# First FFN block of a two-layer transformer kernel: the last six blocks of inner units by quarter products, with the layer norms in the order of the finished tiles

## The chip, the cores and the metric

The kernel runs on one core of one Trainium2 chip, as one launch. The metric is device time in microseconds (us) of that launch; smaller is better. Time before: 1941.02 us, the median of 3 runs (1931.21 to 1941.77).

## What is computed

Two networks follow each other on a sequence of 512 tokens of width 1024. The first has two layers of sliding-window attention, retention and gated linear attention. The second has two layers, each a mixer and a gated FFN with a short convolution, and each followed by a layer norm over the sum with the residual. The change is in the first FFN of the second network, and what comes after it is the odd mixer.

```
def conv_ffn(x, w_up, conv_w, conv_b, w_down):       # D_FF = 2816 = 22 blocks of 128
    a, g = jnp.split(x @ w_up, 2, axis=-1)
    g = conv(g, conv_w) + conv_b                      # depthwise, 3 taps, causal
    return (jax.nn.gelu(g) * a) @ w_down

for l in range(2):
    y = even_mixer(x, ...) if l % 2 == 0 else odd_mixer(x, ...)
    x = layer_norm(alpha * x + y, ln_g[l, 0], ln_b[l, 0])
    y = conv_ffn(x, ffn_w_up[l], ...)
    x = layer_norm(alpha * x + y, ln_g[l, 1], ln_b[l, 1])
```

All matmuls of this part are float32 products made of float32r pieces: an operand is split into a rounded high part and the rest (`hi`, `lo`), and one product costs three matmuls (hi·hi, hi·lo, lo·hi).

## The kernel before

**Tiling.** Tokens stand in four tiles of 128 (t = 0 to 3). The residual sum `z[t]` is 128x1024 and is updated in two column halves n = 0, 1 of 512. `hT` holds the transposed, split input of a stage (8 blocks of 128 features). The 22 blocks of inner units go in three parts of 8, 8 and 6 (`for part, (nch, quart) in enumerate(...)`, line 1481). For each part, the "up" products of at most four blocks at a time are made (the loop `for q0 in range(0, nch, 4)`; 24 matmuls of 128x512 for the g half of each block and 24 for the a half, by `fsteps`, lines 1060 to 1062), then evacuated by `ev_g` (lines 1575 to 1579) and `ev_a` (line 1582), and then the "down" product of the part is added into `z`.

**Two forms of the down product.** With `quart` set (parts 0 and 1) `quarters` (lines 1496 to 1502) builds from each pair of blocks four combined operands, and `down_quart` (from line 1505) forms the product of a pair of blocks, two halves of tokens and two halves of columns as 7 products instead of 8 (a Winograd form of the 2x2 block scheme). Its weights come as three buffers `bq` per pair (x, y, s). A buffer is loaded by SP (line 1517), split into a `w` tile by ACT and DVE (lines 243 and 244, called from `operand`), and then, where `then` is given, the next combination is made in place by a DMA that adds to it, issued on POOL's queue (line 1525). Buffer y goes through four contents in that way, x through three, s holds one. Products run in the order 0, 1, 4, 2, 5, 6, 3 (lines 1547 to 1549); `take` (line 1537) adds a finished one to `z`. Products 0, 5, 6 and 3 share two PSUM banks (`X`), so that some of them hold sums that are taken several times.

Without `quart` (part 2, six blocks) ACT and DVE only split the activations (lines 1588 and 1589), twelve weight tiles are loaded (`load_w`, lines 226 and 227), and `down_part` makes 6 x 3 matmuls for each of four tiles and two halves: 144 matmuls (`dsteps`, lines 231 to 233), each tile's sum taken by line 1621.

**The end of the block.** `ln_stats` (line 1142) reads each half of a finished tile, and `ln_apply` combines the statistics (line 1146), has POOL raise the variance to the power -1/2 (`rpow`, lines 281 and 282), and writes the normed tile by two DVE instructions per half (lines 1151 and 1152). Then `finish` puts off two transposes (`to_T`, line 274, with its split into `hT` by lines 243 and 244) and stores the tile. `start_odd` loads the first weights of the odd mixer (8 tiles of 128x312, three DMA pieces each) and gives a function `Vd(t)` with 24 matmuls of 128x312 for tile t. Before the change the work stands in this order: half n = 0 of tiles 3, 2, 1, 0; half n = 1 of tiles 3, 2, 1, each with its layer norm; Vd(3); half n = 1 of tile 0; Vd(2), Vd(1), Vd(0).

**What sets the order.** Each engine runs its instructions in the order of its own queue and waits for semaphores. The order within a queue is set when the program is built, by a scheduler that moves instructions of the source text past each other. Weight tiles `w` rotate through nine slots (`wslots`: six, and three more inside the FFN, `more_w`), the four `raw` buffers and the eight `bq` buffers are rings of their own. A split of a weight waits until the matmuls that used its slot are done.

## Time and profile before

| | |
|---|---|
| three timed runs | 1931.21, 1941.02, 1941.77 us (median 1941.02) |
| the profiled execution, its own time | 1936.26 us |
| span of the profile | 1934.5 us |
| TensorE (PE) busy | 1874.2 us, 97% |
| VectorE (DVE) busy | 1251.6 us, 65% |
| ScalarE (ACT) busy | 828.1 us, 43% |
| GpSimd (POOL) busy | 260.1 us, 13% |
| the chain that ended last, PE's share | 65% |

The profile is one execution. Its rows have a start in us from the span's start, a length, the engine, the source line and what was written from what. A bracket at the end of a row is the idle time of the engine just before it, and who ended it. In tables by stretch, "x" is the count of instructions, "PEclk" the granted share of TensorE's full clock of 2.4 GHz. A matmul's length overlaps with the next one's, so its price is the distance from start to start.

### The profile page before, as it was taken

The page shows a single profiled execution, that of the slowest core. Times are in us where ns is not written, and L with a number is a line of the kernel's source. Part 1 is how long each engine was busy: PE and PEld are TensorE (multiplying, and loading weights), DVE is VectorE, ACT ScalarE, POOL GpSimd, SP SyncE. Part 2 cuts the span into 40 slices and gives each one's busy share as a digit, 9 for nine tenths or more (in the row PEclk, how much of TensorE's full clock was granted, in tenths as well). Part 3 has the DMA queues.
Part 4 walks back from the last instruction along what each step waited for, and adds up shares of the span by engine and source line. Part 5 has one row for each costly group of instructions (what it writes and reads, how often), then busy time and mean ns, then how long its engine had stood idle before and what let it go on. Part 6 is the DMA issues. An engine that isn't in the chain of part 4 may idle for free.

```text
span 1934.5 us, 29305 instructions
## 1 busy us (share of the span) xinstructions
PE 1874.2 (97%) x10144; PEld 1518.6 (79%) x10144; DVE 1251.6 (65%) x3060; ACT 828.1 (43%) x1840; POOL 260.1 (13%) x380
## 2 busy tenths in 40 slices
PE   7899899999999999999999999999999999999997
PEld 4777687877888888868888888788778888888886
DVE  5697886485775244686675674755776776756646
ACT  2432354433463344453443443244665544434341
POOL 3011101012101000101020020101441200200101
PEclk9999999999999999999999999999999999999999
DMA  8535524226124233403373362363114033733632
GB/s 278 173 89 165 150 86 137 86 84 183 44 94 157 73 106 121 153 12 116 117 155 99 91 149 72 117 188 91 42 29 148 24 133 112 154 97 96 134 88 82
DMA packets 139784, 218.76 MB, mean 113 GB/s; under 512 B 21633, under 2 KB 53747, under 8 KB 139636
## 3 DMA queue, kind: packets, MB, share of 16 engines
q1 hardware_dynamic: 130420, 200.11, 33.6%
q0 software_dynamic: 9216, 16.78, 5.2%
q8 instruction: 80, 1.31, 0.3%
q14 instruction: 68, 0.56, 0.1%
HBM read 207.20 MB, written 14.09 MB: 114 GB/s over the span
## 4 chain that ended last, share of the span: by engine, by line
PE 65%; DVE 7%; issue 6%; POOL 3%; DMA 2%; ACT 1%; POOLq 0%; DVEq 0%; SPq 0%; ACTq 0%
PE mm L1060 10%; PE mm L1062 10%; PE mm L1061 9%; PE mm L231 6%; PE mm L233 6%; PE mm L232 6%; PE t L1095 1%; PE o L1547 1%; PE o L1549 1%; PE o L1548 1%; DMA bq<-in_ffn_w_down_dram 1%; PE mm L1547 1%; PE mm L1549 1%; PE mm L1548 1%; PE t L274 1%
## 5 line engine op out<-in xcount | busy, mean ns | idle before, releaser
L227 DVE TENSOR_TENSOR w<-raw,w 128x512 fp32r<-128x512 f32 (+4 forms) x496 | 307.5, 638 | 140.1 <-ACT w L226 138.4
L226 ACT CAST w<-raw 128x512 fp32r<-128x512 f32 (+4 forms) x504 | 284.5, 575 | 239.8 <-PE mm L233 55.9
L1060 PE MATMUL mm<-hT,w 128*128 128x512 f32 x920 | 366.6, 399 | 0.2
L1062 PE MATMUL mm<-hT,w 128*128 128x512 f32 x920 | 361.6, 394 | 0.1
L1061 PE MATMUL mm<-hT,w 128*128 128x512 f32 x920 | 360.7, 392 | 0.0
L231 PE MATMUL mm<-w,hT 128*128 128x512 f32 (+3 forms) x704 | 278.3, 396 | 1.4 <-ACT hT L243 1.3
L233 PE MATMUL mm<-w,hT 128*128 128x512 f32 (+3 forms) x704 | 262.5, 373 | 0.4 <-DVE hT L244 0.4
L232 PE MATMUL mm<-w,hT 128*128 128x512 f32 (+3 forms) x704 | 261.0, 371 | 0.1
L1060 PEld LDWEIGHTS mm<-hT,w 128*128 128x128 f32 x920 | 172.9, 188 | 39.7 <-ACT w L226 1.8
L1062 PEld LDWEIGHTS mm<-hT,w 128*128 128x128 f32 x920 | 172.7, 188 | 39.4 <-DVE w L227 1.3
L1061 PEld LDWEIGHTS mm<-hT,w 128*128 128x128 f32 x920 | 172.9, 188 | 35.2
L231 PEld LDWEIGHTS mm<-w,hT 128*128 128x128 f32 x704 | 138.9, 198 | 31.0 <-issue 6.5
L233 PEld LDWEIGHTS mm<-w,hT 128*128 128x128 f32 x704 | 138.8, 197 | 21.9 <-DVE hT L244 1.3
L232 PEld LDWEIGHTS mm<-w,hT 128*128 128x128 f32 x704 | 139.4, 198 | 16.8 <-issue 2.0
L1525 POOL DMA_DIRECT2D bq<-in_ffn_w_down_dram x64 | 56.6, 1280 | 413.0 <-DVE w L244 401.7
L1576 DVE SCALAR_TENSOR_TENSOR g<-mm,cw,g 128x511 f32<-128x511 f32 x44 | 33.0, 749 | 108.5 <-ACT g L1575 108.4
L243 ACT CAST w<-bq 128x512 fp32r<-128x512 f32 x112 | 69.0, 621 | 65.1 <-DMA bq<-in_ffn_w_down_dram 20.2
L1090 ACT ACTIVATE E<-E,nm 128x128 f32<-128x128 f32 (+3 forms) x128 | 71.6, 560 | 45.0 <-DVE nm L1089 42.3
L244 DVE TENSOR_TENSOR w<-bq,w 128x512 fp32r<-128x512 f32 x112 | 75.5, 689 | 15.4 <-ACT w L243 14.8
L1582 DVE TENSOR_TENSOR ge<-ge,mm 128x512 f32<-128x512 f32 x44 | 30.1, 685 | 67.6 <-PE mm L1062 67.5
L1575 ACT ACTIVATE g<-mm,cw 128x512 f32<-128x512 f32 x44 | 34.2, 777 | 79.6 <-PE mm L1062 63.1
L1085 DVE COPY pT<-t 128x512 f32<-128x512 f32 (+3 forms) x84 | 43.0, 512 | 37.8 <-PE t L1280 23.3
(472 smaller groups left out, 3458.3 us busy)
## 6 DMA issues: line engine op xcount, KB each, us to landing
raw<-in_ffn_w_up_dram SPq DMA_DIRECT2D x160, 256.0 KB
rawm<-in_w_mod_dram SPq DMA_DIRECT2D x96, 256.0 KB
raw<-in_w_in_dram SPq DMA_DIRECT2D x80, 256.0 KB
bq<-in_ffn_w_down_dram POOLq DMA_DIRECT2D x64, 256.0 KB, 7.7
raw<-in_ev_w_in_dram SPq DMA_DIRECT2D x48, 256.0 KB
bq<-in_ffn_w_down_dram SPq DMA_DIRECT2D x48, 256.0 KB
raw<-in_w_out_dram SPq DMA_DIRECT2D x32, 256.0 KB
raw<-in_ffn_w_down_dram SPq DMA_DIRECT2D x24, 256.0 KB
```

The lines of the kernel that those rows point to most:

```text
L226: SC.copy(hi, r)
L227: (eng or V).tensor_tensor(lo, r, hi.bitcast(F32), op=OP.subtract)
L231: PE.matmul(ps, hi, w[:, 0, w0:w0 + n], start=first, stop=False)
L232: PE.matmul(ps, hi, w[:, 1, w0:w0 + n], start=False, stop=False)
L233: PE.matmul(ps, lo, w[:, 0, w0:w0 + n], start=False, stop=last)
L243: SC.copy(hi, ps)
L244: V.tensor_tensor(lo, ps, hi.bitcast(F32), op=OP.subtract)
L1060: PE.matmul(ps, wh, hi, start=k == ks[0], stop=False)
L1061: PE.matmul(ps, wh, lo, start=False, stop=False)
L1062: PE.matmul(ps, wl, hi, start=False, stop=k == ks[-1])
L1090: SC.activation(E, E, AF.Exp, scale=scale, bias=nm, accum_out=den)
L1525: GP.dma_start(bufs[name, p], src[then](p), accum_op=OP.add)
```

## The change

For the first FFN only (`l == 0`), part 2 goes by quarters as well, as three pairs of blocks. `down_quart` takes a function `done(t, n)` that it calls after the last take of a half tile, and the layer norm of a tile follows when both its halves are done: tiles 0 and 1 after product 5, tiles 2 and 3 after product 3. `start_odd` and the four `Vd(t)` come after all of it, in the order 0, 1, 2, 3.

```diff
-        for part, (nch, quart) in enumerate(((8, True), (8, True), (6, False))):
+        for part, (nch, quart) in enumerate(((8, True), (8, True), (6, l == 0))):
...
-            def down_quart():
+            def down_quart(done=lambda t, n: None):
...
-                product(1, o2, W, True, True, False, lambda r, ps: take(0, r, False, ps))
+                product(1, o2, W, True, True, False, lambda r, ps: (take(0, r, False, ps), done(r, 0)))
...
-                product(5, o6, X, False, False, True, lambda r, ps: take(1, r, True, ps))
+                product(5, o6, X, False, False, True, lambda r, ps: (take(1, r, True, ps), done(r, 1)))
                 o4 = operand("y")
-                product(6, o7, X, False, False, True, lambda r, ps: take(1, 2 + r, True, ps))
-                product(3, o4, X, False, True, True, lambda r, ps: take(0, 2 + r, False, ps, first))
+                product(6, o7, X, False, False, True, lambda r, ps: (take(1, 2 + r, True, ps), done(2 + r, 1)))
+                product(3, o4, X, False, True, True, lambda r, ps: (take(0, 2 + r, False, ps, first), done(2 + r, 0)))
...
-            if quart:
+            if quart and part < 2:
                 down_quart()
                 c0 += nch
                 continue
             lg = rows(1)
+            if quart:
+                def done(t, n):
+                    if t not in st6:
+                        st6[t] = sm.tile([128, 2, 6], F32, name="st6")
+                        ln_stats(st6[t], z[t], n)
+                        return
+                    ln_stats(st6[t], z[t], n)
+                    ln_apply(st6[t], z[t], lg[0], lg[1], lambda m: finish(t, m))
+                down_quart(done)
+                Vd = start_odd()
+                for t in range(4):
+                    flush(("h", t))
+                    drain(Vd(t))
+                flush()
+                c0 += nch
+                continue
```

How the rows move. The first place is DVE's queue at the start of the last part's down product in the changed kernel. Tiles `w` are weight operands, `ge` the activations of the last pair of blocks, `act_11198` the operand that the first product needs of that pair, `bq_11747` to `bq_11751` the three y buffers and `bq_11838` the first x buffer; "waits DMASW" is a wait for an adding DMA of POOL's queue, and each of these splits follows a cast of the same buffer on ACT's queue, which stands in the same order.

```order
L244 TENSOR_TENSOR w_11800<-bq_11747,w_11800 128x512 [waits DMASW0_49,Activation_49]
L244 TENSOR_TENSOR w_11804<-bq_11749,w_11804 128x512 [waits DMASW1_49,Activation_49]
L1582 TENSOR_TENSOR ge_11634<-ge_11634,mm_11702 128x512 [waits PE_49]
L244 TENSOR_TENSOR w_11808<-bq_11751,w_11808 128x512 [waits DMASW2_49,Activation_49]
L1497 TENSOR_TENSOR ge_11603<-ge_11634,ge_11603 128x256 [waits DVE_49]
L244 TENSOR_TENSOR w_11844<-bq_11838,w_11844 128x512 [waits Activation_49]
L1500 SCALAR_TENSOR_TENSOR g0_11728<-ge_11603 128x256 [waits DVE_49]
L244 TENSOR_TENSOR act_11198<-ge_11603,act_11198 128x512 [waits Activation_49]
```

In part two of the program before, the same place has only the first two of four such splits behind the evacuation of line 1582 and none of them ahead of it; in the changed kernel all three y splits for product 4 stand ahead of the first product's last operand.

The second place is DVE's queue where the layer norms meet the first weights of the odd mixer (`w<-raw 128x312`, line 227). Before, around the norms of tiles 3 and 2 (`z_8189`, `z_8188`):

```order
L227 TENSOR_TENSOR w<-raw,w 128x312 [waits DMAHW1_49,DMAHW7_49,DMAHW0_49,Activation_49]
L227 TENSOR_TENSOR w<-raw,w 128x312 [waits DMAHW3_49,DMAHW4_49,DMAHW2_49,Activation_49]
L1621 SCALAR_TENSOR_TENSOR z_8189<-z_8189,mm 128x512 [waits PE_49]
L1142 BN_STATS st_11797<-z_8189 128x6 [waits DVE_49]
L1146 BN_AGGR mv<-st_11797 128x2 [waits DVE_49]
L1151 SCALAR_TENSOR_TENSOR z_8189<-z_8189,mv,lng 128x512 [waits DVE_49]
```

In the changed kernel, at the end of the norm of tile 2 and through that of tile 3:

```order
L1152 SCALAR_TENSOR_TENSOR z_8188<-z_8188,rstd,lnb 128x512 [waits DVE_49]
L1142 BN_STATS st_11996<-z_8189 128x6
L227 TENSOR_TENSOR w<-raw,w 128x312 [waits DMAHW5_49,DMAHW3_49]
L1146 BN_AGGR mv<-st_11996 128x2 [waits DVE_49]
L227 TENSOR_TENSOR w<-raw,w 128x312 [waits DMAHW7_49,DMAHW6_49,DMAHW0_49]
L1151 SCALAR_TENSOR_TENSOR z_8189<-z_8189,mv,lng 128x512 [waits DVE_49]
L1151 SCALAR_TENSOR_TENSOR z_8189<-z_8189,mv,lng 128x512
L1152 SCALAR_TENSOR_TENSOR z_8189<-z_8189,rstd,lnb 128x512 [waits DVE_49,Pool_49]
L1152 SCALAR_TENSOR_TENSOR z_8189<-z_8189,rstd,lnb 128x512 [waits DVE_49]
L227 TENSOR_TENSOR w<-raw,w 128x312 [waits DMAHW3_49,DMAHW2_49,DMAHW1_49]
L227 TENSOR_TENSOR w<-raw,w 128x312 [waits DMAHW7_49,DMAHW6_49,DMAHW5_49]
```

Before, three of the eight splits stand ahead of the first norm and the other five are spread between the norms. Now one stands ahead of the norms (in tile 0's), the second and third come in tile 3's norm, the fourth and fifth behind it, and the last three come between the splits of `hT` that follow.

The third place is PE's queue after the last product, where Vd(0) begins (`mm_12118` is Vd(0), `mm_12161` Vd(1), `w_12066` and `w_12073` the first two of the eight weight tiles):

```order
L231 MATMUL mm_12118<-w_12066,hT_82 128x312 [waits Activation_49]
L232 MATMUL mm_12118<-w_12066,hT_82 128x312
L274 MATMUL t_12119<-con_72,z1_8187 128x128 [waits DVE_49,PE_49]
L274 MATMUL t_12119<-con_72,z1_8187 128x128 x3
L233 MATMUL mm_12118<-w_12066,hT_82 128x312
L231 MATMUL mm_12118<-w_12073,hT_82 128x312
L231 MATMUL mm_12161<-w_12066,hT_82 128x312 [waits Activation_49]
L274 MATMUL t_12126<-con_72,z1_8187 128x128 [waits DVE_49]
L274 MATMUL t_12126<-con_72,z1_8187 128x128 x3
L232 MATMUL mm_12161<-w_12066,hT_82 128x312
L232 MATMUL mm_12118<-w_12073,hT_82 128x312 [waits DVE_49]
```

Here PE's queue, which held 18 matmuls of a down product between two tiles' Vd before, holds only transposes and Vd matmuls, and the second weight's low part (the last row) stands ahead of 89 of the 96 Vd matmuls. The queue of PE has 7736 rows for 7755 before.

## Rows read from the trace of the kernel before

**Rows 1.** The page's head: span, busy time, share and instructions of PE and DVE.
```profile
span 1934.5 us, 29305 instructions
PE 1874.2 (97%) x10144; PEld 1518.6 (79%) x10144; DVE 1251.6 (65%) x3060; ACT 828.1 (43%) x1840; POOL 260.1 (13%) x380
```

**Rows 2.** Busy time by stretch: down product of part two, up of part three, its down, Vd.
```profile
core 0: us, PE busy (x) PEld busy (x) DVE busy (x) ACT busy (x) POOL busy (x), PEclk, DMA share, GB/s
1112.60:1151.00 38.40, 38.40 (x167) 31.16 (x167) 29.91 (x49) 18.68 (x33) 10.57 (x12) 1.00 0.77 159
1151.00:1217.38 66.38, 66.38 (x291) 54.23 (x290) 31.07 (x55) 25.86 (x48) 0.00 (x0) 1.00 0.29 87
1217.38:1246.61 29.23, 29.23 (x127) 23.61 (x126) 19.81 (x32) 5.42 (x10) 3.14 (x4) 1.00 0.36 103
1246.61:1270.20 23.59, 22.80 (x147) 20.34 (x146) 19.58 (x39) 10.10 (x23) 3.78 (x7) 1.00 0.38 123
```

**Rows 3.** PE's waits from 1100 to 1300 us: total, times, longest.
```profile
PE mm L233 <- DVE hT L244: 0.4, 1, 0.4
PE mm L231 <- ACT hT L243: 0.2, 1, 0.2
```

**Rows 4.** PE in time: first matmuls of both down products, ends of both, last Vd.
```profile
1112.42 0.40 PE L1547 MATMUL o<-w,act 128*128 128x512 f32 x1
...
1151.28 0.39 PE L1060 MATMUL mm<-hT,w 128*128 128x512 f32 x1
...
1217.38 0.39 PE L231 MATMUL mm<-w,act 128*128 128x512 f32 x1
...
1266.78 0.30 PE L231 MATMUL mm<-w,hT 128*128 128x312 f32 x1
...
1270.20 0.39 PE L1060 MATMUL mm<-hT,w 128*128 128x512 f32 x1
```

**Rows 5.** DVE groups from 1217.38 to 1270.2 us: count, busy us, mean ns, idle before.
```profile
L1151 DVE SCALAR_TENSOR_TENSOR z<-z,mv,lng 128x512 f32<-128x512 f32 x8 | 5.7, 748 | 0.1
L1152 DVE SCALAR_TENSOR_TENSOR z<-z,rstd,lnb 128x512 f32<-128x512 f32 x8 | 5.7, 747 | 1.8 <-POOL rstd L282 1.8
L1142 DVE BATCH_NORM_STATS2 st<-z 128x6 f32<-128x512 f32 x8 | 5.5, 692 | 0.2
L1621 DVE SCALAR_TENSOR_TENSOR z<-z,mm 128x512 f32<-128x512 f32 x8 | 5.5, 682 | 5.9 <-PE mm L233 5.9
L244 DVE TENSOR_TENSOR hT<-t,hT 128x512 fp32r<-128x512 f32 x8 | 5.4, 683 | 1.5 <-ACT hT L243 1.5
L1146 DVE BATCH_NORM_AGGREGATE mv<-st 128x2 f32<-128x12 f32 x4 | 0.8, 207 | 0.1
```

**Rows 6.** DVE in time: splits of weights, and the last evacuation of part two.
```profile
1108.45 4.88 DVE L244 TENSOR_TENSOR w<-bq,w 128x512 fp32r<-128x512 f32 x7 [0.19 <-ACT w L243]
1113.24 0.68 DVE L1582 TENSOR_TENSOR ge<-ge,mm 128x512 f32<-128x512 f32 x1
...
1254.42 0.87 DVE L227 TENSOR_TENSOR w<-raw,w 128x312 fp32r<-128x312 f32 x2
```

**Rows 7.** PE transposes from 1217.38 to 1270.2 us: the group's busy time.
```profile
L274 PE MATMUL t<-con,z 128*128 128x128 f32 x32 | 4.8, 273 | 0.0
```

**Rows 8.** POOL's adding DMAs: issues in time, then all 64, issue to landing.
```profile
1109.44 2.64 POOL L1525 DMA_DIRECT2D bq<-in_ffn_w_down_dram  x3 [12.96 <-DVE w L244]
...
DMA to landing us min/median/max: 3.9/7.7/10.8
```

**Rows 9.** ACT in time, part two: the two casts that an adding DMA held up.
```profile
1117.13 0.62 ACT L243 CAST w<-bq 128x512 fp32r<-128x512 f32 x1 [0.57 <-DMA bq<-in_ffn_w_down_dram]
1119.37 0.62 ACT L243 CAST w<-bq 128x512 fp32r<-128x512 f32 x1 [1.61 <-DMA bq<-in_ffn_w_down_dram]
```

**Rows 10.** Stretches around two pauses of PE in the first network.
```profile
160.50:164.00 3.50, 1.50 (x9) 1.34 (x10) 2.09 (x7) 0.47 (x1) 1.20 (x2) 0.88 0.02 8
164.00:167.50 3.50, 3.50 (x7) 2.10 (x8) 2.26 (x10) 0.00 (x0) 0.00 (x0) 0.50 0.22 75
167.50:171.00 3.50, 3.50 (x16) 2.89 (x14) 1.77 (x4) 0.38 (x1) 0.84 (x2) 0.65 0.47 116
...
181.50:185.00 3.50, 1.90 (x13) 1.40 (x11) 3.13 (x10) 0.37 (x1) 0.00 (x0) 1.00 0.48 150
185.00:188.50 3.50, 3.31 (x17) 2.17 (x18) 3.50 (x8) 0.62 (x1) 0.00 (x0) 1.00 0.55 128
```

## The prediction

> **What bounds the kernel now.** I read the page's head first: TensorE (PE) is busy for 97% of the span and DVE for 65% [rows 1]. Then the busy times of the stretches around the change: in the last part's up product, its down product and Vd, PE leaves 0.8 us of 119 us free, and the table of PE's waits has 0.6 us in 200 us [rows 2, 3]. So in this place the kernel is bound by PE's work, and every matmul taken away is worth its distance from start to start, as long as no wait opens. Next to that the reader should see how far DVE is loaded: 31.07 us of 66.38 in the up stretch, but 19.58 of 23.59 in the stretch with the layer norms and Vd [rows 2]. There DVE has little left, and whatever moves onto it there, or is squeezed into a shorter stretch, can become the bound. Last I read the adding DMAs, since the changed part waits for twelve of them, which the trace shows in parts one and two alone [rows 8, 9].
>
> **The work of PE.** The down product of part two is 168 matmuls from 1112.42 to 1151.28 [rows 4], 0.231 us each. The last part had 144 such matmuls and gets 7 x 3 x 2 x 3 = 126: 18 fewer, **-4.2 us**. The transposes (32, 4.8 us [rows 7]) and the 96 matmuls of Vd stay. Vd's price is 24 matmuls from 1266.78 to 1270.20 [rows 4], 0.1425 us each.
>
> **Edits that I cost at nothing.** `quarters` gives DVE and ACT more to do for three pairs of blocks in the up stretch, where DVE is free for 35 of 66 us [rows 2]; were that cover gone, the operands of the first product would come later, which is the next step. Eight `bq` loads now stand in SP's queue ahead of most of the last part's up weights. In part two the loads stand like that already, and PE had no idle time in its 38.40 us [rows 2]. The twelve weight loads of before become nine loads and twelve adding DMAs of the same size, in stretches with a DMA share of 0.29 to 0.36 [rows 2]. POOL has to issue twelve more DMAs, and the four norms' two POOL steps stand behind them, but the last issue is due two products earlier than the first norm.
>
> **A wait at the first product.** The first product needs the high part of operand m of the last pair after 14 matmuls, 3.2 us. On ACT and DVE the splits for product 4 stand ahead of it, the third of them behind the landing of the third adding DMA (the first place of the order). In part two the corresponding issues begin at 1109.44 and the third of a run of them about 0.7 us after the second [rows 8]; the second stands for the third here, as one of the three is made early in both. That is 2.3 us before the product's start at 1112.42 [rows 4]. The shortest landing is 3.9 us [rows 8], and the casts held up at 1117.13 and 1119.37 [rows 9] show 7 us and more after issue, when four x loads ran beside them; here one does. So the data is there 1.6 to 4.7 us after the product's start. A cast, a split, the evaluation of line 1497 and the cast of m follow, 2.2 us with the lengths of [rows 6, 9]. m is ready at 3.8 to 6.9 us where 3.2 was wanted: a wait of 0.6 to 3.7 us, and nothing if the DMA lands earlier than any did. I take **+2.0 us**, the middle. The Trainium skill, "DMA: Bandwidth & Descriptors", section "Anatomy of one DMA — SWDGE (gpsimd) path", gives a DMA of this path about 2.0 us and its bytes at 436 GB/s, an estimate of 2.6 us for 256 KB; by it this wait would be nothing and the sum 2.0 us less. The trace disagrees: none of its 64 adding DMAs landed in under 3.9 us [rows 8].
>
> **The tail, where DVE takes over.** Before, tiles finish one after the other, 4 to 5 us apart, and DVE does their norms beside 72 matmuls of the second half and Vd. Now the first norm can begin only after product 5 and the last after product 3, the last product. Until product 5 ends PE needs 90 x 0.231 + 2.0 = 22.8 us from its start; DVE has some 30 instructions of 0.4 to 0.7 us in that time, 18 us, and keeps up. From there DVE's queue holds, up to the split of the eighth weight tile of Vd: all 16 applies (5.7 + 5.7), 6 of 8 statistics and 6 of 8 takes (0.75 x (5.5 + 5.5)), the combining (0.8), the splits of `hT` (5.4) [rows 5], and eight splits of 128x312 at 0.87 / 2 [rows 6], 3.5: together **29.3 us**, which DVE has to do in one run. PE has in the same time two products (36 x 0.231 = 8.3), the transposes (4.8) and those matmuls of Vd whose operands are there. It can't run ahead, because its queue holds Vd(0) and Vd(1) behind the low parts of weight tiles 2 to 8, and DVE's queue holds these behind the norms of tiles 0 to 2 and partly of tile 3 (the second and third place of the order). Behind the eighth split 55 matmuls of Vd are left, 7.8 us. So the next stage begins 22.8 + 29.3 + 7.8 = 59.9 us after the first matmul of the down product. Before, it was 1270.20 - 1217.38 = 52.8 us [rows 4].
>
> That gives **+7.1 us**: PE's saving of 4.2 is in it, and the waits that open are worth 11.3. Bounds of the tail: DVE's rows overlap when they follow each other without a wait (seven splits in 4.88 us [rows 6], 0.70 each, but 0.61 where none waits), so 1 us less is possible; and DVE can begin at the first half of product 5, 1 us earlier. With no wait at the first product the low end is +7.1 - 2.0 - 2.0 = +3.1. Upward, the wait of 3.7 instead of 2.0, and DVE arriving 3 us late at the first norm because a late adding DMA holds up a split ahead of it, make +11.8.
>
> What hides the rest of the change: the transposes of the odd mixer's first weights and its loads come as before, behind Vd's last matmuls, and 16 us of tail give the loads more time than they had. If a load is late next, it is the seventh and eighth weight of Vd, which stand in SP's queue behind the store of tile 3.
>
> **Against the clock of the runs.** The sum is made against the profiled execution's own 1936.26 us: 1943.4. That execution lies 4.8 below the median of the three runs and 5.1 above the lowest; the mean of all four is 1937.6, 1.3 above it. I predict **1944.7 us**. A measurement of this kernel can tell about 0.5%, 9.7 us, from no change.
>
> **The rivals.**
>
> *The saving comes through.* If PE finds its operands in time as it did before, only -4.2 us remains: 1937.6 - 4.2 = 1933.4. For it: PE waited 0.6 us in 200 us [rows 3], and the two earlier parts run by quarters without idle time [rows 2]. Against it: after those parts comes an up product with nothing for DVE to finish, here a norm and eight splits of new weights. It decides if DVE's run after product 5 stays under PE's own 26.8 - 7.8 = 19 us; 29.3 counted from rows would have to be a third too high. Chance 0.12.
>
> *The chain of adding DMAs.* Buffer y takes four contents in a row, and each needs a split, an issue and a landing. A median landing of 7.7 us and 1.3 us for split and issue is 9.0 us a link; product 5 wants the third content 16.4 us and product 3 the fourth 24.6 us after the first. Where landings stay near the median this just fits. With 10.8, the longest [rows 8], the third content comes some 3 us and the fourth 3 us later still, and as the splits stand ahead of the norms in DVE's queue, it costs PE and DVE both: 6 to 7 us on top, 1951. For it: landings of 7 us and more in part two; against it: the pairs are three, so that a link moves a quarter less, and the DMA share is lower. Chance 0.13.
>
> *The clock of TensorE.* PE now pauses some 3.5 us in one piece while DVE finishes tiles 2 and 3. In the first network a stretch of 3.5 us with 1.50 us busy was followed by 7 us at half the clock (0.50 and 0.65); one with 1.90 was not [rows 10]. If the fall comes here, part of Vd runs at 1.2 GHz: at most 24 of its matmuls outside DVE's shadow, 3.4 us more, 1948. The Trainium skill, "TensorE: Matmul & The Clock Gate", section "What's actually happening", says that activity releases the throttle and an idle stretch brings it back; by that rule the pause suffices. The two stretches of the trace show it falling in one of two cases. Chance 0.15, half of it beyond 0.5%.
>
> *The change does nothing.* The order shows the rows moved and PE's queue 19 rows shorter; I leave it out.
>
> **How the numbers follow.** The forecast has 0.58, the three rivals 0.12, 0.13 and 0.15, and 0.02 is left for a gain that I don't see. The forecast's own range is +3.1 to +11.8 on 1937.6, 1941 to 1949. Taking in the spread of the runs and the rivals up to 2 in 10 left out, the range is 1934 to 1956. Faster by over 0.5% (below about 1931): 0.02. Slower by over 0.5%: the DMA chain 0.13, half of the clock 0.07, the forecast's upper end 0.05: 0.25. Within: 0.73.
>
> **What would show it.** In the profile after: the down product of the last part with 126 matmuls; a wait of PE of 1 to 4 us, some 3 us after its first matmul; DVE without idle time for nearly 30 us from the end of product 5; PE waiting for line 227 or 244 in Vd, some 9 us in all, at full clock; and the first matmul of line 1060 about 60 us after the start. It is wrong if PE's waits in this place sum to less than 5 us, if they lie before product 5 rather than behind it, or if the time is lost outside these 60 us.

## The result, and the profile after

The changed kernel takes 1951.26 us in the median of 12 runs (1945.8 to 1956.96), against 1940.93 us for the kernel before, run beside it: a ratio of **1.0056, 95% interval 1.0041 to 1.0072**, so some 11 us slower (8 to 14). The forecast was 1944.7 us with a range of 1934 to 1956.

The loss lies in the place that the prediction named. From the first matmul of the last part's down product to the next stage's first matmul of line 1060 it was 52.8 us [rows 4], and now it is 1284.76 - 1222.18 = 62.6 us; a second profile of the changed kernel gave 63.0. The rest of the span is 1881.7 us before, and 1887.8 and 1881.3 in the two profiles after; most of that spread lies far ahead of the change, since the last part's up product begins at 1151.28 us before and at 1156.08 and 1147.64 in the two profiles after. So the experiments below are compared by this place, and the 9.8 us of it are the loss.

The page's head, the lines that answer to [rows 1]:

```profile
span 1950.4 us, 29343 instructions
PE 1876.7 (96%) x10126; PEld 1521.0 (78%) x10126; DVE 1268.5 (65%) x3093; ACT 836.1 (43%) x1855; POOL 268.0 (14%) x392
```

PE has 18 matmuls fewer and yet 2.5 us more busy time; DVE has 16.9 us more. The place by stretch, as in [rows 2]: the columns are PE, weight load, DVE, ACT and POOL busy, then the granted clock, the DMA share and GB/s.

```profile
core 0: us, PE busy (x) PEld busy (x) DVE busy (x) ACT busy (x) POOL busy (x), PEclk, DMA share, GB/s
1222.18:1225.40 3.22, 3.22 (x15) 2.44 (x13) 1.07 (x3) 0.62 (x1) 0.86 (x1) 1.00 1.04 207
1225.40:1228.10 2.70, 0.15 (x1) 0.00 (x0) 2.10 (x5) 1.78 (x4) 1.57 (x2) 1.00 0.87 134
1228.10:1232.00 3.90, 3.87 (x10) 3.08 (x11) 3.16 (x7) 2.47 (x5) 1.01 (x2) 0.56 0.90 126
1232.00:1247.50 15.50, 15.50 (x68) 12.28 (x66) 12.70 (x21) 6.10 (x11) 4.38 (x5) 1.00 0.62 94
1247.50:1258.50 11.00, 9.67 (x45) 7.67 (x45) 10.96 (x21) 2.62 (x6) 1.50 (x4) 1.00 0.23 79
1258.50:1265.00 6.50, 2.40 (x15) 1.65 (x14) 6.50 (x12) 1.17 (x2) 0.73 (x2) 1.00 0.14 57
1265.00:1269.00 4.00, 1.77 (x7) 1.21 (x7) 3.99 (x9) 0.29 (x1) 1.39 (x2) 0.62 0.67 205
1269.00:1272.50 3.50, 3.50 (x15) 3.42 (x16) 1.77 (x4) 0.21 (x2) 0.00 (x0) 0.50 0.73 220
1272.50:1284.76 12.26, 12.26 (x88) 12.08 (x87) 6.42 (x16) 6.52 (x16) 0.32 (x2) 0.99 0.32 88
```

Three things are to be seen. PE stands still for nearly the whole second stretch, and runs at 0.56 of its clock in the third. From 1247.5 (the end of product 5) to 1269 DVE is busy without a gap: 10.96 of 11.00, 6.50 of 6.50, 3.99 of 4.00 us, where PE has 2.40 of 6.50. And behind that PE runs at half its clock again. PE's waits from 1217 to 1290 us, the view that had 0.6 us in it before [rows 3]:

```profile
PE mm L232 <- DVE w L227: 5.2, 2, 3.1
PE o L1547 <- ACT act L243: 2.6, 1, 2.6
PE o L1547 <- DVE z L1537: 0.8, 1, 0.8
PE t L274 <- DVE hT L244: 0.8, 1, 0.8
PE o L1547 <- DVE mv L1146: 0.5, 1, 0.5
PE mm L231 <- ACT hT L243: 0.4, 1, 0.4
```

They sum to 10.3 us, 7.7 of it behind product 5. With this **the loss adds up**: 18 matmuls less are -4.2 us, waits of 10.3 instead of 0.6 are +9.7, and the slow clock costs 3.87 x 0.44 = 1.7 us in the stretch from 1228.1 and 1.77 x 0.38 + 3.50 x 0.50 = 2.4 us in the two from 1265. That makes +9.6, and the place says +9.8. This is a count of where PE's time went and not yet what each part would give back: the first 0.7 of the 2.4 us lies ahead of a wait that ends when DVE is done (1268.85), and at full clock that wait would have been longer.

The first wait, on the queues of POOL, ACT and PE (views of the timeline; the second POOL row is the latter half of the first):

```profile
1219.20 1.75 POOL L1525 DMA_DIRECT2D bq<-in_ffn_w_down_dram  x2 [2.50 <-DVE w L244]
...
1219.90 1.05 POOL L1525 DMA_DIRECT2D bq<-in_ffn_w_down_dram  x1
```
```profile
1223.85 0.62 ACT L243 CAST w<-bq 128x512 fp32r<-128x512 f32 x1 [2.22 <-DMA bq<-in_ffn_w_down_dram]
1225.75 1.14 ACT L243 CAST w<-bq 128x512 fp32r<-128x512 f32 x2 [1.28 <-DMA bq<-in_ffn_w_down_dram]
1227.46 1.14 ACT L243 CAST act<-ge 128x512 fp32r<-128x512 f32 x2 [0.57 <-DVE ge L1497]
```
```profile
1222.18 0.39 PE L1547 MATMUL o<-w,act 128*128 128x512 f32 x1
...
1225.16 0.39 PE L1548 MATMUL mm<-w,yT 128*128 128x512 f32 x1
1228.13 0.55 PE L1547 MATMUL o<-w,act 128*128 128x512 f32 x1 [2.59 <-ACT act L243]
...
1265.19 0.41 PE L232 MATMUL mm<-w,hT 128*128 128x312 f32 x1 [3.11 <-DVE w L227]
...
1268.85 0.63 PE L232 MATMUL mm<-w,hT 128*128 128x312 f32 x1 [2.04 <-DVE w L227]
...
1284.76 0.39 PE L1060 MATMUL mm<-hT,w 128*128 128x512 f32 x1
```

POOL issues the second and third adding DMA at 1219.20 and 1219.90; ACT's casts of what they bring wait until 1223.85 and 1225.75, and only behind the second of them come the evaluation of line 1497 and, at 1227.46, the cast of operand m, for which PE waits until 1228.13. That is the chain of the prediction, link by link. The tail, on DVE's queue:

```profile
1247.02 0.69 DVE L244 TENSOR_TENSOR w<-bq,w 128x512 fp32r<-128x512 f32 x1 [0.75 <-ACT w L243]
...
1264.67 0.47 DVE L227 TENSOR_TENSOR w<-raw,w 128x312 fp32r<-128x312 f32 x1
...
1270.09 0.68 DVE L244 TENSOR_TENSOR hT<-t,hT 128x512 fp32r<-128x512 f32 x1
1273.06 1.53 DVE L244 TENSOR_TENSOR hT<-t,hT 128x512 fp32r<-128x512 f32 x2 [2.29 <-ACT hT L243]
...
1276.25 0.48 DVE L227 TENSOR_TENSOR w<-raw,w 128x312 fp32r<-128x312 f32 x1
```

From 1247.02 to 1270.8 no row on DVE has an idle bracket: 23.8 us. The second weight split, which PE needs for its seventh matmul of Vd, comes at 1264.67 in the norm of tile 3, as the order said, and the eighth ends at 1276.73.

### The profile page after: what moved, and what is told of

It is laid out like the page before. It is cut to its first block, busy times and chain, and to the rows that moved or that the text cites. A ratio compares the mean times of both kernels' runs of the same rounds, so it can differ in the third digit from the quotient of the medians.

```text
span 1950.4 us, 29343 instructions
## 1 busy us (share of the span) xinstructions
PE 1876.7 (96%) x10126; PEld 1521.0 (78%) x10126; DVE 1268.5 (65%) x3093; ACT 836.1 (43%) x1855; POOL 268.0 (14%) x392
## 4 chain that ended last, share of the span: by engine, by line
PE 56%; issue 11%; DVE 7%; DMA 4%; POOL 3%; ACT 2%; POOLq 0%; DVEq 0%; ACTq 0%; SPq 0%
PE mm L1060 8%; PE mm L1062 8%; PE mm L1061 8%; PE mm L231 5%; PE mm L233 5%; PE mm L232 5%; DMA bq<-in_ffn_w_down_dram 3%; PE t L1095 1%; POOL bq L1525 1%; PE o L1547 1%; PE o L1549 1%; PE o L1548 1%; PE t L274 1%; DVE w L227 1%; PE o L1962 1%
## 5 line engine op out<-in xcount | busy, mean ns | idle before, releaser
L227 DVE TENSOR_TENSOR w<-raw,w 128x512 fp32r<-128x512 f32 (+4 forms) x484 | 300.5, 638 | 140.3 <-ACT w L226 138.3
L226 ACT CAST w<-raw 128x512 fp32r<-128x512 f32 (+4 forms) x492 | 277.7, 574 | 229.0 <-PE mm L233 42.7
L1525 POOL DMA_DIRECT2D bq<-in_ffn_w_down_dram x76 | 67.1, 1254 | 510.8 <-DVE w L244 487.0
L243 ACT CAST w<-bq 128x512 fp32r<-128x512 f32 x133 | 81.9, 621 | 85.3 <-DMA bq<-in_ffn_w_down_dram 33.1
L244 DVE TENSOR_TENSOR w<-bq,w 128x512 fp32r<-128x512 f32 x133 | 89.3, 688 | 23.2 <-ACT w L243 22.6
```

What stands on the lines that cost most here:

```text
L226: SC.copy(hi, r)
L227: (eng or V).tensor_tensor(lo, r, hi.bitcast(F32), op=OP.subtract)
L243: SC.copy(hi, ps)
L244: V.tensor_tensor(lo, ps, hi.bitcast(F32), op=OP.subtract)
L1525: GP.dma_start(bufs[name, p], src[then](p), accum_op=OP.add)
```

## The experiments

Three questions were open. Is it the adding DMAs that make the first wait, and do they cost more further on? Is the tail DVE's amount of work, or only the place of eight splits in its queue? And what is the clock's own part? Times of the place in us, from the start of the first matmul of the down product to that of line 1060, and the ratio of the run times to the kernel before:

| run | start, end | place | waits | slow clock | ratio of the runs, 95% interval |
|---|---|---|---|---|---|
| before | 1217.38, 1270.20 | 52.8 | 0.6 | 0 | |
| the change | 1222.18, 1284.76 | 62.6 | 10.3 | 4.1 | 1.0056 (1.0041 to 1.0072) |
| the change, second profile | 1213.74, 1276.75 | 63.0 | 10.7 | 4.0 | 1.0062 (1.0033 to 1.0092) |
| no adding DMAs | 1222.00, 1278.01 | 56.0 | 5.9 | 2.6 | 1.0024 (1.0007 to 1.0042) |
| m first | 1222.46, 1282.95 | 60.5 | 8.4 | 4.2 | 1.0042 (1.0018 to 1.0067) |
| od weights early | 1221.81, 1282.87 | 61.1 | 9.8 | 3.4 | 1.0047 (1.0024 to 1.0070) |
| half norm | 1217.91, 1271.63 | 53.7 | 5.3 | 0 | 1.0029 (1.0012 to 1.0045) |
| half norm, again | 1223.58, 1277.99 | 54.4 | 5.9 | 0 | 1.0020 (0.9991 to 1.0049) |
| order alone | 1221.08, 1273.07 | 52.0 | 0.9 | 0 | 1.0008 (0.9983 to 1.0033) |
| od splits on POOL | 1224.11, 1284.77 | 60.7 | 9.4 | 3.4 | 1.0058 (1.0034 to 1.0081) |
| queues mended | 1222.03, 1281.98 | 60.0 | 7.7 | 4.3 | 1.0042 (1.0008 to 1.0075) |
| second step off DVE | 1227.10, 1284.74 | 57.6 | 8.4 | 1.7 | 1.0047 (1.0027 to 1.0067) |
| filled pause | 1225.61, 1286.19 | 60.6 | 6.9 | 2.6 | 1.0060 (1.0024 to 1.0095) |
| no DMAs, half norm | 1220.23, 1269.58 | 49.4 | 1.7 | 0 | 0.9993 (0.9969 to 1.0016) |

"Waits" are PE's waits in the place, and "slow clock" is PE's busy time there times the share of the clock that was missing, summed over short stretches. With quarters PE's matmuls take 52.8 - 0.6 - 4.2 = 48.0 us at full clock. These three add up to the place within 0.6 us in every run with quarters (in the filled pause with some 2.9 us of added matmuls); order alone, which has all 144 matmuls, is 1.1 us under its sum.

The place is one profile for each row. The runs by themselves bear out the gain of four edits: no adding DMAs, half norm, order alone, and both causes out. The intervals of the other six overlap widely with the change's, so the gain of 1.5 to 5 us that their places show stands on one profile each. And in all thirteen series the run times differ from the kernel before by 0.5 to 4.7 us more than the places do; where this part is lost the runs don't show.

All edits below are to the changed kernel. First the repeat of it:

> A second profile of the changed kernel, for the spread of the place: 62.6 us in the first. If the waits come from the order of the queues and the DMAs' landing they come again, with the clock's part of 2 to 4 us the only thing that can differ: 59 to 63.5 us. Rival, the first profile was an outlier: under 58 us.

The place took 63.0 us, with the same six waits of 10.7 us together. The place and its waits repeat.

### The adding DMAs

```diff
-                        if then:
+                        if then and part < 2:
                             GP.dma_start(bufs[name, p], src[then](p), accum_op=OP.add)
```

> Leaves out the twelve adding DMAs of the last part's quarter products (part 2 of the first FFN), so that the y and x buffers are split again with the content they have; every split, cast and matmul stays, in the same order. The place is timed from the first matmul of the last part's down product to the next stage's first of line 1060: 62.6 us in the changed kernel, 52.8 before. My theory (the wait at the first product comes from splits of y that wait for an adding DMA ahead of operand m in the queues of ACT and DVE; the tail behind product 5 is DVE's own work): the wait of 2.7 us at the first product and its 1.8 us at half clock go, nothing else does: 58 us, 4.5 us less. Rival, the chain of adding DMAs costs in the later products too: 56 us or less. Rival, the first wait has another cause (the evaluation itself is late): 62 us, as before.

Measured 56.0 us, 6.6 less. PE's waits in the place, all of them:

```profile
PE mm L232 <- DVE w L227: 4.7, 2, 3.1
PE t L274 <- DVE hT L244: 0.8, 1, 0.8
PE mm L231 <- ACT hT L243: 0.4, 1, 0.4
```

The waits for `act`, for the takes and for the combining are gone, and so is the half clock in the down product; the tail's waits stay as they were (4.7 for 5.2 us at line 232). So my theory holds for the cause of the first wait, but its price was set too low and the rival's 56 us is the closer figure: the adding DMAs also delay DVE's splits further on, by the 0.8 us at product 6, the 0.5 us at product 3 (put down to the combining, which stands just behind the take of product 6) and about 1 us more. Could the wait be avoided with the DMAs in? `mi[0]` holds the last pair's two split instructions of m, on ACT and on DVE, and `tc.issue_after` queues what is issued under it behind one of them:

```diff
...
-            act, ops = [], {}
+            act, ops, behind = [], {}, lambda i: tc.issue_after(mi[0][i].ins) if part == 2 else ExitStack()
...
-                split(m[:, 0], m[:, 1], r0)
+                mi[0] = split(m[:, 0], m[:, 1], r0)
...
-                o5 = operand("y", None, (1, 1))
+                with behind(0), behind(1): o5 = operand("y", None, (1, 1))
```

> Same work as the changed kernel; on ACT and DVE the three splits of y for product 4 are queued behind the split of operand m of the last pair. My theory: the wait of 2.7 us at the first product and its half clock go, as without the DMAs: 58 us from first down matmul to line 1060 (62.6 in the changed kernel). Rival, the chain of adding DMAs through buffer y has no room: the later issue of the third and fourth content puts the wait into products 4, 5 or 3 instead, 61 us or more.

Measured 60.5 us, 2.1 less where 4.6 was expected: the rival came nearer. The wait for operand m is gone, and another stands at product 6:

```profile
PE mm L232 <- DVE w L227: 4.9, 2, 3.1
PE o L1547 <- DVE z L1537: 2.9, 1, 2.9
```

Product 6 adds into a bank that `take` of product 5 must have read, and on DVE this take stood behind two splits of y (1243.71 and 1244.98) whose casts waited for adding DMAs. Moved by one place in the queue, the chain of buffer y shows itself at the next take. So there is no slack in that chain for the time of one split.

### DVE's amount behind product 5

```diff
-                    ln_apply(st6[t], z[t], lg[0], lg[1], lambda m: finish(t, m))
+                    mv = sm.tile([128, 2], F32, name="mv")
+                    V.bn_aggr(mv, st6[t].rearrange("p a b -> p (a b)"))
+                    for m in range(2):
+                        hs = slice(512 * m, 512 * m + 512)
+                        V.scalar_tensor_tensor(z[t][:, hs], z[t][:, hs], mv[:, 0:1], lg[0][:, hs], op0=OP.subtract, op1=OP.mult)
+                        finish(t, m)
```

> Leaves out the second step of the four layer norms at the end of the first FFN (line 1152, eight DVE instructions of 0.70 us, and POOL's power for it), all else as in the changed kernel. My theory (DVE's amount behind product 5 sets the end): 5.6 us of DVE's run of 29.7 go, and the end comes 4.5 to 7.5 us earlier, 55 to 58 us from first down matmul to line 1060 (62.6 in the changed kernel). Rival, the time is set by weight loads, by the clock or by waits and not by DVE's work: 61 us or more.

Measured 53.7 us, 8.9 less. The waits:

```profile
PE o L1547 <- ACT act L243: 2.5, 1, 2.5
PE mm L232 <- DVE w L227: 1.9, 3, 1.0
PE o L1547 <- DVE z L1537: 0.9, 1, 0.9
```

5.6 us of DVE's work take PE's wait for line 227 from 5.2 to 1.9 us, and with the pauses the half clock of Vd goes. That is more than the expected 4.5 to 7.5, since the clock also stayed at 1.00 behind the first wait, which has nothing to do with the norms. The run was made once more for that:

> A second profile of the kernel without the second step of the norms: in the first one the clock stayed at 1.00 behind the wait of 2.5 us in the first product, while in the changed kernel it fell behind 2.7 us, and its median lies further above the kernel before than the place accounts for. If DVE's amount is the cause and the clock a matter of the single run: 53.7 us again, or up to 56 where the clock falls at the first pause, and still no pause of more than 2 us in Vd. Rival, the first profile was a lucky one and the tail is no shorter: 60 us or more.

54.4 us, with a first wait of 3.2 us and again no fall behind it. The ratios of the two series (0.29 and 0.20%, some 5.6 and 3.9 us) are above what the places say (+0.9 and +1.6 us), the first by a little more than its interval; the profiled execution of the first series was the fastest of its ten, and its granted clock over the whole execution, 0.993, the highest (0.983 to 0.990 in the others). Whether the others lost their clock in this place is not shown. Then both at once:

> Leaves out both the twelve adding DMAs of the last part and the second step of the four layer norms of the first FFN. If the adding DMAs and DVE's amount behind product 5 are together all that stood against the saving: 52.8 - 4.2 = 48.6 us is the floor of PE's work, and some wait for the weight splits that come late in DVE's queue (1.9 us when only the half norm was out) stays: 48.6 to 51 us from first down matmul to the next stage's up matmuls. Rival, a third cost is left (products waiting on each other through the shared banks X, or the loads of Vd's weights): 52 us or more.

Its edit is the first and the third diff together. Measured 49.4 us, in the expected range, at the clock of 1.00 throughout and with one wait left:

```profile
PE mm L232 <- DVE w L227: 1.7, 3, 1.0
```

So the 18 matmuls do save 4.2 us (48.0 us of matmuls and this wait make 49.7), and the adding DMAs and DVE's amount are the two things that stood against it. Is it the place of the splits in the queue rather than the amount?

```diff
-                o4 = operand("y")
+                o4, vd[0] = operand("y"), start_odd() if part == 2 else None
...
-                Vd = start_odd()
+                Vd = vd[0]
```

> Same work as the changed kernel; start_odd is called ahead of product 6 rather than after product 3, which puts the eight splits of its weights on DVE ahead of the norms of tiles 2 and 3. My theory (the amount of DVE work behind product 5 sets the end): DVE's run stays near 30 us, but behind its last instruction only one tile's 24 matmuls of Vd are left instead of 55, 4 us less, and the pauses of PE are shorter, so that less of Vd is at half clock: 57 to 59 us from first down matmul to line 1060 (62.6 in the changed kernel). Rival, only the late place of the splits costs: PE's waits of 5.2 us for line 227 and the half clock behind them go without anything in their place: 55 us or less. Rival, the splits put ahead of the norms delay the transposes as much as they gain: 62 us.

Measured 61.1 us. The first wait was 1.1 us longer: the third adding DMA was issued 2.3 us before the product, as in the changed kernel, and took 6.9 us to land instead of 5.8, the longest of the twelve in each run. SP's queue holds the same loads up to there, so about 60 otherwise: less gain than my theory expected, and far from the 55 of the rival that only the place costs.

```profile
PE o L1547 <- DVE z L1537: 4.5, 2, 3.7
PE o L1547 <- ACT act L243: 3.7, 1, 3.7
```

The wait for line 227 is gone, and 3.7 us stand at product 3 instead, which waits for the take of product 6: that take now came behind tile 1's norm and five of the splits (at 1258.24). So in this order too DVE has more to do there than PE has cover for.

### The order of the norms without the quarters

```diff
-        for part, (nch, quart) in enumerate(((8, True), (8, True), (6, l == 0))):
+        for part, (nch, quart) in enumerate(((8, True), (8, True), (6, False))):
...
                 for t in (3, 2, 1, 0):
                     down_part(1, w[1], t)
-                    if t == 1:
-                        flush(("h", 3))
-                        drain(Vd(3))
-                for t in (2, 1, 0):
+                for t in (3, 2, 1, 0):
```

> The second half of the change without the first: the last part keeps its 144 matmuls (no quarters), but all four tiles' layer norms come ahead of all of Vd in the program. Timed from the first matmul of the last part's down product to the next stage's first of line 1060 (52.8 us before, 62.6 in the changed kernel). My theory (the cost comes from the norms that all begin behind product 5, close to the end): here tiles still finish 4 to 5 us apart, so the norms keep their cover and only the last tile's norm is bare: 53 to 56 us. Rival, putting Vd behind all the norms is what costs, whatever the products: 59 us or more.

Measured 52.0 us, below the 53 to 56 expected and 0.8 below the kernel before, a difference that the runs can't show (1.0008). One wait of 0.9 us is all there is:

```profile
PE t L274 <- DVE hT L244: 0.9, 1, 0.9
```

Putting Vd behind all the norms costs nothing as long as tiles finish 4 to 5 us apart. The cost comes with the quarters: they finish two tiles at product 5 and two at product 3, and bring DVE nine more splits of weights and six more takes.

### The clock

```diff
+                        if part == 2 and i == r == 0 and p == 2:
+                            pf = ps_t().rearrange("p a b -> p (a b)")
+                            for _ in range(12):
+                                PE.matmul(pf, L[0][0][:, 0], ws[0][:, 0], start=True, stop=True, skip_group_check=True)
```

> The changed kernel with twelve matmuls of 128x512 (2.8 us) into an unused bank, their result thrown away, put on PE's queue where it waits for operand m in the first product; all else in the same order. They fit into the wait of 2.7 us. If the fall of the clock behind that pause has its price in the time (ten matmuls took 4.0 us there where 2.3 are due): the clock stays at 1.00 and the place takes 1.7 us less, 61 us from first down matmul to the next stage's up matmuls (62.6 in the changed kernel). Rival, the slow stretch behind the pause has another cause, or the time lost there is made up before product 5 ends: 62.6 us as before, or more.

Measured 60.6 us, 2.0 less. The added matmuls are line 1550 here, and line 1551 is line 1547 of the others:

```profile
1228.35 2.88 PE L1550 MATMUL t<-w,act 128*128 128x512 f32 x12
1231.42 0.50 PE L1551 MATMUL o<-w,act 128*128 128x512 f32 x1 [0.19 <-ACT act L243]
```

Operand m comes as late as before, PE is busy until then, and the granted clock is 1.00 in this stretch and up to Vd. So the fall behind the first pause is due to the pause and has a price of its own, 2.0 us by this profile, 1.7 by the count above; the run times (1.0060 against 1.0056) are too coarse to show it. In Vd the clock was not tested by itself.

### Can DVE be relieved?

```diff
-        ws = {k: load_w(w_in, 128 * k, 0, 312, pieces=((896, 128), (1152, 152), (1944, 32))) for k in K8}
+        ws = {k: load_w(w_in, 128 * k, 0, 312, pieces=((896, 128), (1152, 152), (1944, 32)), eng=GP) for k in K8}
```

> The changed kernel, with the low parts of the odd mixer's eight first weights (line 227, 128x312) made by POOL instead of DVE. My theory (DVE's amount and its order behind product 5): DVE's run loses 3.5 us, PE's waits for those low parts (5.2 us) go, the wait at the first product (2.6 us) stays: 55 to 58 us from first down matmul to line 1060 (62.6 in the changed kernel). Rival, PE then waits as long for the transposes of tiles 2 and 3, as when the splits were put ahead of the norms: 60 to 62 us. Rival, POOL is too slow for the splits (its 128x512 subtraction takes 1.33 us, so some 0.8 us each): the wait for line 227 stays, with POOL as its end.

Measured 60.7 us: the first rival. PE waits for tiles 2 and 3 instead (3.2 us for the second step of the norm and 2.6 for the split of `hT`, against 5.2 for line 227), and DVE's rows grew:

```profile
L1152 DVE SCALAR_TENSOR_TENSOR z<-z,rstd,lnb 128x512 f32<-128x512 f32 x8 | 6.8, 890 | 1.6 <-POOL rstd L282 1.6
L1151 DVE SCALAR_TENSOR_TENSOR z<-z,mv,lng 128x512 f32<-128x512 f32 x8 | 6.3, 832 | 0.0
```

They had 745 and 746 ns in the changed kernel. The steps' 1.9 us more and the new wait of 1.6 us for `rstd` are together about what the eight splits had taken on DVE (3.7 us). The next run put all mended queues together, the edit of m first, the one above and this one, `behind(None)` being behind the last take on DVE:

```diff
...
-                product(5, o6, X, False, False, True, lambda r, ps: (take(1, r, True, ps), done(r, 1)))
-                o4 = operand("y")
-                product(6, o7, X, False, False, True, lambda r, ps: (take(1, 2 + r, True, ps), done(2 + r, 1)))
+                product(5, o6, X, False, False, True, lambda r, ps: take(1, r, True, ps))
+                with behind(None): o4 = operand("y")
+                done(0, 1), done(1, 1), product(6, o7, X, False, False, True, lambda r, ps: (take(1, 2 + r, True, ps), done(2 + r, 1)))
```

> The changed kernel with the weight splits of Vd on POOL, the y splits for product 4 queued behind operand m, and the y splits for product 3 queued on DVE behind the takes of product 5 and in the program ahead of the norms of tiles 0 and 1. Same work. My theory: no wait at the first product, none at product 6; DVE has behind product 5 29.3 - 3.5 + 1.9 (three y splits) = 27.7 us, then 24 matmuls of Vd (3.4 us) and the last split's way: 20.8 + 27.7 + 4.5 = 53 us, range 52 to 55, from first down matmul to line 1060 (52.8 before). Rival, the third and fourth content of buffer y still land too late, and PE waits for them in product 5 or 3: 56 us or more.

Measured 60.0 us against 53 expected. The first wait is gone and no wait for an adding DMA replaces it, but the transposes wait 5.6 us for the norms. Where POOL's splits run beside the norms, on DVE and on POOL:

```profile
1250.03 1.33 DVE L1152 SCALAR_TENSOR_TENSOR z<-z,rstd,lnb 128x512 f32<-128x512 f32 x1 [1.66 <-POOL rstd L282]
1251.29 1.33 DVE L1151 SCALAR_TENSOR_TENSOR z<-z,mv,lng 128x512 f32<-128x512 f32 x1
```
```profile
1249.98 4.60 POOL L227 TENSOR_TENSOR w<-raw,w 128x312 fp32r<-128x312 f32 x4
```

A step of the norm that takes 0.75 us takes 1.33, a split on POOL 1.15 in the mean, and the norm waits 1.66 us for its `rstd` because POOL's splits stand ahead of it. My theory of DVE's amount had left out that the two engines slow each other: 1.2 us over the sixteen steps, with waits of 2.5 us for `rstd` where the changed kernel has none. It had left out the clock as well, 4.3 us of the 60.0 (table). The last one is this run with more taken off DVE; `E` is true for tiles 0 to 2 of this FFN:

```diff
...
-            V.scalar_tensor_tensor(z[:, hs], z[:, hs], rstd, b[:, hs], op0=OP.mult, op1=OP.add)
+            (SC.mul(z[:, hs], z[:, hs], rstd), GP.tensor_tensor(z[:, hs], z[:, hs], b[:, hs], op=OP.add)) if E else V.scalar_tensor_tensor(z[:, hs], z[:, hs], rstd, b[:, hs], op0=OP.mult, op1=OP.add)
```

> As the run before, and the second step of the norms of tiles 0 to 2 goes to ACT (times rstd) and POOL (plus bias) instead of DVE: six DVE instructions of 0.70 us less. My theory: 4.2 us less of DVE's run, 49 to 51 us from first down matmul to line 1060, under the 52.8 of the kernel before; in the median 0 to 4 us below it. Rival, the longer way of a half tile (0.6 on ACT and 1.33 us on POOL instead of 0.70) delays the transposes and Vd: 53 us or more.

Measured 57.6 us, again the rival: PE waits 7.5 us at the transposes for POOL's additions, with DVE's first step at 1095 ns and POOL's addition at 1348 in the mean:

```profile
L1151 DVE SCALAR_TENSOR_TENSOR z<-z,mv,lng 128x512 f32<-128x512 f32 x8 | 8.5, 1095 | 0.0
```
```profile
L1152 POOL TENSOR_TENSOR z<-z,lnb 128x512 f32<-128x512 f32 x6 | 8.0, 1348 | 1.7 <-ACT z L1152 1.7
```

No version with quarters in the last part came under the place of the kernel before while it did the whole work.

## Why the prediction was right in its mechanism and short in its size

- **The time.** 1951.3 us is 6.6 above the forecast of 1944.7. Of this 3.3 are the base (1937.6 taken, 1940.9 measured beside the change), 2.7 the place (+9.8 where +7.1 was forecast), and the rest lies outside it. The result is above the forecast's own range, 1941 to 1949, and inside 1934 to 1956 by what was added for the spread and the rivals. "Slower by over 0.5%", which came about by a little, had a chance of 0.25.
- **PE's saving, -4.2 us.** Right: 49.4 us with both causes out, where 48.0 of matmuls and the one wait of 1.7 make 49.7.
- **What was costed at nothing.** Right ahead of the down product: with `quarters` and the eight `bq` loads in it the up product takes 1222.18 - 1156.08 = 66.1 us, and before it took 1217.38 - 1151.28 = 66.1.
- **The wait at the first product, +2.0 us, range 0.6 to 3.7.** It was 2.6 us, by the chain that was given. The third DMA was issued 2.3 us before the product's start, as expected, and the cast of what it brought began 3.6 us after it (1.6 to 4.7 expected). The page of the Trainium skill that was weighed there, "DMA: Bandwidth & Descriptors", section "Anatomy of one DMA — SWDGE (gpsimd) path", would have made this wait nothing by the estimate of 2.6 us. The trace disagrees here too; over the twelve adding DMAs of this part it has:

```profile
DMA to landing us min/median/max: 4.0/4.6/5.8
```

- **The tail, 29.3 us of DVE, then 55 matmuls.** The three terms 22.8 + 29.3 + 7.8 measured 25.3 + 29.2 + 8.0: product 5 ended at 1247.5, the eighth split at 1276.7. So nearly all of the excess lies in the first term, as 0.6 us more wait and 1.7 us of slow clock. The second is met by luck, two errors that cancel: DVE's rows overlap by more than the 1 us that was allowed, so that its run without a gap was 23.8 us, and the 3.0 us of gaps behind it came from PE, whose transposes of tile 3 came late, behind matmuls at half clock, and ran at half clock too.
- **The step that was mis-sized: the clock had no term in the sum.** It stood as a rival, for one pause of 3.5 us in Vd and at most 3.4 us. It fell behind both pauses, the first of them only 2.6 us, and cost 1.7 to 2.0 and about 2.4 us. The waits that opened were 10.3 - 0.6 = 9.7 us where 11.3 was forecast, and with these 4.1 us the forecast's +7.1 becomes +9.6, where 9.8 was measured. "At full clock" in what would show it was wrong.
- **The chain of adding DMAs, chance 0.13.** It doesn't run away as the rival had it, with a median landing of 4.6 us and not 7.7. But it isn't free either: the last adding DMA is issued at 1240.88 and lands 5.4 us later, the split of what it brings (1247.02) stands ahead of the take of product 5 on DVE, and product 6 waits 0.8 us for that take. By the first experiment the chain costs some 2 us behind the first product, where the rival had 6 to 7, and by the second it has no slack.
- **The saving comes through, 0.12.** It needed DVE's run under 19 us; it was 23.8 without a gap.
- **The place.** Of the 10.3 us of waits 2.6 lie before product 5 ends and 7.7 behind it, 6.4 of those in Vd and its transposes where 9 were forecast.

## What to carry to other kernels

A form with fewer matmuls needs time on the engine that prepares its operands and takes its results; here that engine had none left, and 4.2 us saved became 9.8 lost. Count that engine's rows in the stretch where the last results fall, not over the span, and count what the form adds to them. And a pause of the matmul engine has two prices in a sum, the wait and the slow matmuls behind it; the second belongs into the sum wherever the trace shows it at comparable pauses, not among the rivals.

## What was not expected of the hardware

**DVE and POOL slow each other by what they read.** In the run with the mended queues two steps of the norm, whose two tensors are in SBUF, took 1.33 us beside POOL's subtractions (1250.03 and 1251.29, above), where they take 0.75 alone. In the same stretch the statistics at 1252.54, which read one tensor from SBUF, took 0.68 us, and the take at 1253.91, which reads one from SBUF and one from PSUM, 0.63; in the changed kernel the means are 0.68 and 0.66. POOL paid too: its 128x312 split took 0.84 us where DVE was at statistics and a take (in the run with the second step off DVE, the first row below), and 1.15 in the mean of the four beside the norm. Not each step pays: the second row, of the mended queues, begins while POOL is at a split.

```profile
1255.40 0.84 POOL L227 TENSOR_TENSOR w<-raw,w 128x312 fp32r<-128x312 f32 x1
```
```profile
1253.14 0.73 DVE L1152 SCALAR_TENSOR_TENSOR z<-z,rstd,lnb 128x512 f32<-128x512 f32 x1
```

The Trainium skill, "SBUF — State Buffer", section "Who interferes with whom", says that a DVE instruction with two SBUF inputs contends with a POOL instruction that reads SBUF, and that one with a single SBUF input doesn't, some fast modes apart. The trace agrees on both counts, and here POOL, though it stands idle, relieved DVE of little in the stretch with the norms.

**The clock behind a pause is not told by the pause's length alone.** At the same place in the first product the granted clock fell behind waits of 2.5, 2.6, 2.6 and 3.7 us (the change twice, POOL's splits, od weights early), and stayed at 1.00 behind 2.5 and 3.2 us in the two profiles with the half norm. The stretch behind the wait of 2.5 us, beside 0.56 in the changed kernel's third stretch above:

```profile
1223.90:1228.00 4.10, 4.10 (x18) 3.30 (x19) 4.10 (x9) 3.11 (x7) 0.86 (x1) 1.00 0.90 136
```

The Trainium skill, "TensorE: Matmul & The Clock Gate", section "What's actually happening", has an idle stretch bring the throttle back; the filled pause agrees that it is the idling, and which of these pauses count stays open.
